# Feed-forward gate and up projections as seven half-width products (one level of Strassen's scheme), with sums made by accumulating DMA

## Chip, cores and metric

One core of one Trainium2 chip runs the kernel. The metric is the time of one execution in device microseconds. Three timed runs of the kernel before gave 751.33, 752.55 and 753.04 us; their median is 752.55 us.

## What is computed

One block of a streaming encoder on 512 tokens of width 1024, in float32. The change touches the last two steps; attention and gates before them stay as they are.

```python
x = x + jnp.einsum('bsd,de->bse', merged, w_out[layer])

h2 = _rmsnorm(x, g_ffn[layer])
ff = jax.nn.silu(jnp.einsum('bsd,df->bsf', h2, w_ffn_gate[layer])) * \
    jnp.einsum('bsd,df->bsf', h2, w_ffn_up[layer])
x = x + jnp.einsum('bsf,fd->bsd', ff, w_ffn_down[layer])
```

`w_ffn_gate` and `w_ffn_up` are 1024 x 2816, `w_ffn_down` is 2816 x 1024.

## The kernel before

Activations lie transposed: 128 features on the partitions, 512 tokens along the row, so a matrix of width 1024 is 8 tiles (k-tiles). Each float32 factor is split in two float32r parts: ScalarE copies it into the high part (L86), VectorE subtracts that from the factor for the low part (L87). `mm3` (L204 to L206) multiplies with three matmuls: high by high, high by low, low by high.

Weights come through `Stream`: a 128 x 1024 tile is loaded by SyncE's queue into a `raw` slot (6 of them, 5 tiles ahead), split into `wh` and `wl` (4 slots each, 2 tiles ahead) and used for 24 matmuls of 128 x 128 weights by 512 tokens. The stages, in the order of time:

- attention, with projections that fill the gaps, and the branch projections;
- the output projection (w_out): eight columns d, 24 matmuls each. VectorE adds the residual (`xr`, L701), ScalarE scales the sum by `g_ffn` into `h2h` (L705), VectorE makes `h2l` (L706), ScalarE squares it (L709), GpSimd sums the squares (L713);
- the feed-forward: 22 pairs n; each is a gate tile and an up tile, 24 matmuls each. After the first gate tile a matmul of the squares with ones gives the norm; ScalarE takes the root (L722), VectorE the reciprocal `r2` (L723). Per pair VectorE multiplies gate and up by `r2` (L726, L728), ScalarE applies SiLU (L727), GpSimd multiplies the two (L729), and the result is split into `fh` and `fl`;
- the down projection: eight columns of 66 matmuls over the 22 tiles, residual added (L740), output stored (L741).

A scheduler sets the order of the instructions on each engine; each engine and each DMA queue then runs its own in that order. In PSUM there are two pools of four banks: `pc` and `pt` tiles rotate through one, all others through the other.

Of the kernel before, what the change touches and what calls it, by code (L numbers as in the profile page):

```python
# [42 lines left out]
def block_kernel(  # L43
# [22 lines left out]
    small = ctx.enter_context(tc.tile_pool(name="small", bufs=4))  # L66
# [17 lines left out]

    def split(h, l, src):
        a = nc.scalar.copy(out=h, in_=src)  # L86
        b = nc.vector.tensor_tensor(out=l, in0=src, in1=f(h), op=ALU.subtract)  # L87
        return a, b

    def pinned(instrs):  # L90
        for ins in instrs:
            tc.keep_in_program_order(ins)

    class Stream:
        AHEAD, SPLIT = 5, 2
# [58 lines left out]
    srcs += [w_out[d] for d in range(8)]
    for n in range(NF):
        srcs += [w_fg[n], w_fu[n]]
    for d in range(8):
        srcs += [w_dn[d, :, 0:1024], w_dn[d, :, 1024:2048], w_dn[d, :, 2048:2816]]

    ws = Stream(srcs)  # L160
# [41 lines left out]
    def mm3(ps, w, a, first, last):  # L202
        (wh, wl), (ah, al) = w, a
        nc.tensor.matmul(out=ps, lhsT=wh, rhs=ah, start=first, stop=False)  # L204
        nc.tensor.matmul(out=ps, lhsT=wh, rhs=al, start=False, stop=False)  # L205
        nc.tensor.matmul(out=ps, lhsT=wl, rhs=ah, start=False, stop=last)  # L206
# [38 lines left out]
    def full_ct(acts, **kw):  # L245
        ps = kw.pop("ps", None) or PS("pc")
        drain(proj_ct(ps, acts, **kw))
        return ps
# [443 lines left out]
        split(h, l, gA[d])  # L692
        mg.append((h, l))

    x2, h2 = [], []
    acc = None
    for d in range(8):
# [4 lines left out]
        x2.append(xr)  # L702
        h, l = B(F32R, "h2h"), B(F32R, "h2l")
        gc = g_ffn[:, d : d + 1]
        nc.scalar.activation(out=h, in_=xr, func=AF.Copy, scale=gc)  # L705
        nc.vector.scalar_tensor_tensor(out=l, in0=xr, scalar=gc, in1=f(h), op0=ALU.mult, op1=ALU.subtract)  # L706
        h2.append((h, l))
# [9 lines left out]
    for n in range(NF):
        pg = full_ct(h2)
        if n == 0:
            pn = PS("pn2")  # L720
            nc.tensor.matmul(out=pn, lhsT=ones[:, 0:P], rhs=acc, start=True, stop=True)
            nc.scalar.activation(out=r2, in_=pn, func=AF.Sqrt, scale=1.0 / D, bias=epst)  # L722
            nc.vector.reciprocal(out=r2, in_=r2)  # L723
        pu = full_ct(h2)
        t1, t2 = B(name="t1"), B(name="t2")
        nc.vector.tensor_tensor(out=t1, in0=pg, in1=r2, op=ALU.mult)  # L726
        nc.scalar.activation(out=t1, in_=t1, func=AF.Silu)  # L727
        nc.vector.tensor_tensor(out=t2, in0=pu, in1=r2, op=ALU.mult)  # L728
        nc.gpsimd.tensor_tensor(out=t1, in0=t1, in1=t2, op=ALU.mult)  # L729
# [12 lines left out]


# [60 lines left out]
```

## Time and profile before

| | us |
|---|---|
| median of three runs | 752.55 |
| profiled execution, first to last instruction (span) | 751.0 |
| TensorE busy (matmul) | 738.1 |
| VectorE busy | 431.8 |
| ScalarE busy | 325.1 |
| GpSimd busy | 103.0 |

The profile is of one execution; its span is the time from the first instruction to the last. Engines: PE is TensorE's matmuls, PEld its weight loads, DVE VectorE, ACT ScalarE, POOL GpSimd, SP SyncE. A duration that is given for a matmul overlaps with the next one's, so the distance between two starts tells what one costs.

### The profile page before, as it was taken

How to read it: one execution, taken by the hardware profiler on the slowest of the kernel's cores; microseconds unless marked ns; L12 is line 12 of the kernel's file. 1: busy time of each engine (PE TensorE's matmuls, PEld its weight loads, DVE VectorE, ACT ScalarE, POOL GpSimd, SP SyncE). 2: the span in 40 equal slices, each digit the busy share in tenths (PEclk: the TensorE clock that was granted, in tenths of full speed). 3: DMA queues.
4: the chain of work that ended last, by engine and by line, in shares of the span. 5: the costliest groups of instructions: out<-in, count | busy, mean ns of one | idle time of the engine just before them, and what ended most of it. 6: DMA issues, size and time to landing. Idle time of an engine off the chain costs nothing.

```text
span 751.0 us, 9018 instructions
## 1 busy us (share of the span) xinstructions
PE 738.1 (98%) x3406; PEld 611.6 (81%) x3406; DVE 431.8 (57%) x648; ACT 325.1 (43%) x514; POOL 103.0 (14%) x139
## 2 busy tenths in 40 slices
PE   8999999999989999999999999999999999999998
PEld 6887887888878878888888888888888888888886
DVE  5856877766687887987446454445545533232220
ACT  6633566877566676544444232323232222222110
POOL 0067000000023223300321011101101111000000
PEclk9999999999999999999999999999999999999999
DMA  8622121211121111244432322332232323333200
GB/s 316 218 98 84 59 83 56 81 61 58 57 84 43 46 39 42 73 152 170 161 120 84 113 84 93 105 103 94 85 112 86 98 83 105 103 118 117 64 14 29
DMA packets 23803, 71.12 MB, mean 95 GB/s; under 512 B 2768, under 2 KB 3408, under 8 KB 23760
## 3 DMA queue, kind: packets, MB, share of 16 engines
q1 hardware_dynamic: 23472, 70.40, 28.0%
q8 instruction: 27, 0.44, 0.2%
q10 hardware_dynamic: 288, 0.15, 0.1%
q14 instruction: 16, 0.13, 0.1%
HBM read 68.44 MB, written 2.10 MB: 94 GB/s over the span
## 4 chain that ended last, share of the span: by engine, by line
PE 89%; DVE 3%; POOL 3%; ACT 2%; issue 2%; DMA 0%; DVEq 0%; POOLq 0%; ACTq 0%
PE pc L204 24%; PE pc L205 24%; PE pc L206 24%; PE pt L221 6%; PE pk L221 3%; PE sc L395 1%; PE sc L394 1%; POOL qn L300 1%; DVE wl L87 1%; PE tb L400 1%; ACT wh L86 1%; PE ta L400 1%; PE av L555 1%; POOL qn L314 1%; PE av L556 1%
## 5 line engine op out<-in xcount | busy, mean ns | idle before, releaser
L86 ACT CAST wh<-raw 128x1024 fp32r<-128x1024 f32 (+2 forms) x136 | 130.9, 963 | 299.1 <-PE pc L205 165.4
L87 DVE TENSOR_TENSOR wl<-raw,wh 128x1024 fp32r<-128x1024 f32 (+2 forms) x136 | 172.7, 1270 | 105.3 <-ACT wh L86 101.2
L204 PE MATMUL pc<-h2h,wh 128*128 128x512 f32 x352 | 137.3, 390 | 0.0
L206 PE MATMUL pc<-h2h,wl 128*128 128x512 f32 x352 | 137.0, 389 | 0.0
L205 PE MATMUL pc<-h2l,wh 128*128 128x512 f32 x352 | 136.9, 389 | 0.0
L204 PE MATMUL pc<-hh,wh 128*128 128x512 f32 x192 | 76.6, 399 | 1.9 <-DVE vs L363 1.5
L205 PEld LDWEIGHTS pc<-h2l,wh 128*128 128x128 f32 x352 | 66.1, 188 | 14.1 <-issue 0.2
L204 PEld LDWEIGHTS pc<-h2h,wh 128*128 128x128 f32 x352 | 66.1, 188 | 14.0 <-issue 0.2
L206 PEld LDWEIGHTS pc<-h2h,wl 128*128 128x128 f32 x352 | 66.1, 188 | 13.5
L206 PE MATMUL pc<-hh,wl 128*128 128x512 f32 x192 | 75.5, 393 | 0.0
L205 PE MATMUL pc<-hl,wh 128*128 128x512 f32 x192 | 75.3, 392 | 0.0
L204 PE MATMUL pc<-fh,wh 128*128 128x512 f32 x176 | 68.5, 389 | 0.0
L205 PE MATMUL pc<-fl,wh 128*128 128x512 f32 x176 | 68.5, 389 | 0.0
L206 PE MATMUL pc<-fh,wl 128*128 128x512 f32 x176 | 68.5, 389 | 0.0
L729 POOL TENSOR_TENSOR t<-t,t 128x512 f32<-128x512 f32 x22 | 30.0, 1363 | 208.5 <-DVE t L728 121.0
L728 DVE TENSOR_TENSOR t<-pc,r 128x512 f32<-128x512 f32 x22 | 15.2, 691 | 67.0 <-PE pc L206 63.2
L204 PEld LDWEIGHTS pc<-hh,wh 128*128 128x128 f32 x192 | 36.4, 190 | 9.2 <-issue 1.7
L206 PEld LDWEIGHTS pc<-hh,wl 128*128 128x128 f32 x192 | 36.2, 189 | 7.8
L205 PEld LDWEIGHTS pc<-hl,wh 128*128 128x128 f32 x192 | 36.4, 190 | 6.7
L530 POOL TENSOR_SCALAR_AFFINE_SELECT om<-om 128x128 f32<-128x128 f32 x32 | 11.4, 356 | 210.4 <-DVE obl L87 138.3
L204 PEld LDWEIGHTS pc<-fh,wh 128*128 128x128 f32 x176 | 33.0, 188 | 6.9
L206 PEld LDWEIGHTS pc<-fh,wl 128*128 128x128 f32 x176 | 33.0, 188 | 6.9
(204 smaller groups left out, 1166.4 us busy)
## 6 DMA issues: line engine op xcount, KB each, us to landing
raw<-w_fg_dram SPq DMA_DIRECT2D x22, 512.0 KB, 3.2
raw<-w_fu_dram SPq DMA_DIRECT2D x22, 512.0 KB, 3.2
raw<-w_gate_dram SPq DMA_DIRECT2D x16, 512.0 KB, 3.2
raw<-w_dn_dram SPq DMA_DIRECT2D x16, 512.0 KB, 3.5
raw<-w_tc_dram SPq DMA_DIRECT2D x12, 512.0 KB, 4.5
raw<-w_ct_dram SPq DMA_DIRECT2D x8, 512.0 KB, 3.3
raw<-w_br_dram SPq DMA_DIRECT2D x16, 256.0 KB, 2.6
raw<-w_out_dram SPq DMA_DIRECT2D x8, 512.0 KB, 3.3
```

Source lines behind the costliest of these rows:

```text
L86: a = nc.scalar.copy(out=h, in_=src)
L87: b = nc.vector.tensor_tensor(out=l, in0=src, in1=f(h), op=ALU.subtract)
L204: nc.tensor.matmul(out=ps, lhsT=wh, rhs=ah, start=first, stop=False)
L205: nc.tensor.matmul(out=ps, lhsT=wh, rhs=al, start=False, stop=False)
L206: nc.tensor.matmul(out=ps, lhsT=wl, rhs=ah, start=False, stop=last)
L221: nc.tensor.matmul(out=pss[tb], lhsT=hx[:, tb * P : (tb + 1) * P], rhs=wx[:, wsl], start=(kt == 0 and i == 0), stop=(kt == KT - 1 and i == 2),
L300: nc.gpsimd.tensor_tensor(out=q3, in0=q3, in1=gqkt[:, gi : gi + 1, :].broadcast_to([P, 8, 64]), op=ALU.mult,)
L314: nc.gpsimd.tensor_tensor(out=q3[:, :, 0:16], in0=t1, in1=t2, op=ALU.add)
L400: nc.tensor.transpose(out=ps[:, off + (tb - sb) * P : off + (tb - sb + 1) * P], in_=tiles[tb][:, sb * P : (sb + 1) * P], identity=ident,)
L530: nc.gpsimd.affine_select(out=t[:, o + w - P : o + w], in_=t[:, o + w - P : o + w], pattern=[[-1, P]], compare_op=ALU.is_gt, fill=fill, ba ...
L728: nc.vector.tensor_tensor(out=t2, in0=pu, in1=r2, op=ALU.mult)
L729: nc.gpsimd.tensor_tensor(out=t1, in0=t1, in1=t2, op=ALU.mult)
```

## The change

Gate and up tile of a pair are taken together. Tokens are halved (256 each), features are halved (4 k-tiles each), and the pair is a 2 x 2 block matrix with gate and up as its columns. Winograd's form of Strassen's scheme makes the four blocks of the result with seven products (`PRODUCTS`) where there are eight; each has 4 k-tiles x 3 matmuls on 256 tokens. In exchange sums are formed:

- of the activations, once, in the output projection's stage: `s13`, `s24`, beside the plain halves `a1x`, `a2x`. Its columns run in the order 0, 4, 1, 5, 2, 6, 3, 7; x after the residual goes to a scratch in DRAM and is read back for the end;
- of the weights, per pair: T1 and T3 (`t13`) by two plain loads of SyncE's queue and one accumulating DMA of GpSimd's queue from DRAM; T2 and T4 by VectorE (`sums`);
- of the products, by ScalarE (two copies) and VectorE (`c11`, `middle`, `c21`, `gate`).

For the up tile, and for the w_out tiles, the low part is no subtraction of VectorE: ScalarE writes the negated high part into `wl`, and an accumulating DMA of GpSimd's queue adds the raw tile to it. In the pair loop the order on TensorE, VectorE and ScalarE is the program's order. Pair 0 runs k-tiles 0 to 2 of all products first, then k-tile 3. `r2` multiplies the gate alone; the up part gets it at the very end (`yo`). GpSimd computes nothing there. All 22 results are split after the loop. `raw` has 5 slots in place of 6, `small` 3 in place of 4; weights are loaded 4 tiles ahead.

```diff
-N_BLK, N_RAW, N_SPLIT = 66, 6, 4
+N_BLK, N_RAW, N_SPLIT = 66, 5, 4
...
+    def split_dma(h, l, src):
+        nc.scalar.copy(out=h, in_=src)
+        nc.scalar.mul(out=l, in_=src, mul=-1.0)
+        nc.gpsimd.dma_start(out=l, in_=src, accum_op=ALU.add)
...
+        def load_t(self):
+            n = self.n
+            self.t13 = tsum.tile([P, 2 * S], F32, tag="t13", name=f"t13_{n}")
+            nc.sync.dma_start(out=self.t13[:, lo_w], in_=w_fu[n, :, lo_w])
+            nc.sync.dma_start(out=self.t13[:, hi_w], in_=w_fg[n, :, hi_w])
+            nc.gpsimd.dma_start(
+                out=self.t13.rearrange("p (a b) -> p a b", b=S),
+                in_=w_fg[n, :, lo_w].unsqueeze(1).broadcast_to([P, 2, S]), accum_op=ALU.add,
+            )
...
+        def sums(self):
+            self.t2, self.t4 = B(name="tb2"), B(name="tb4")
+            tt(self.t2, self.t13[:, lo_w], self.g)
+            tt(self.t4, self.t2, self.u[:, hi_w])
...
+    PRODUCTS = {
+        1: ("b11", "a11"), 2: ("b21", "a12"), 5: ("t1", "s1"), 7: ("t3", "s3"),
+        6: ("t2", "s2"), 4: ("t4", "a22"), 3: ("b22", "s4"),
+    }
+
+    def product(ps, pair, i, kts=range(KT // 2)):
+        w, x = PRODUCTS[i]
+        wh, wl = pair.of(w)
+        for kt in kts:
+            sl = slice(kt * P, (kt + 1) * P)
+            mm3(ps[:, 0:half], (wh[:, sl], wl[:, sl]), x_of[x](kt), kt == 0, kt == KT // 2 - 1)
...
+            if n == 0:
+                for i in PRODUCTS:
+                    product(o.ps(i), w, i, range(3))
+                for i in PRODUCTS:
+                    product(o.m[i], w, i, range(3, 4))
+                pn = PS("pn2")
+                nc.tensor.matmul(out=pn, lhsT=ones[:, 0:P], rhs=acc, start=True, stop=True)
+                nc.scalar.activation(out=r2, in_=pn, func=AF.Sqrt, scale=1.0 / D, bias=epst)
+                nc.vector.reciprocal(out=r2, in_=r2)
+            else:
+                product(o.ps(1), w, 1)
+                prev.gate()
+            if w1:
+                w1.sums()
+            if prev:
+                prev.mul()
+            o.copy(1, lo_t)
+            if n:
+                product(o.ps(2), w, 2)
+            o.c11()
+            if w1:
+                w1.prep_13()
+                w1.prep_g()
+            if n:
+                product(o.ps(5), w, 5)
+            o.copy(5, hi_t)
+            if w2:
+                w2.load_g()
+            if n:
+                product(o.ps(7), w, 7)
+                product(o.ps(6), w, 6)
+            o.middle()
+            if w1:
+                w1.high_24()
+            if n:
+                product(o.ps(4), w, 4)
+            o.c21()
+            if w1:
+                w1.low_24()
+            if n:
+                product(o.ps(3), w, 3)
+            if w2:
+                w2.prep_u()
+            if w3:
+                w3.load_u()
+            prev = o
...
+    for t in ff:
         h, l = B(F32R, "fh"), B(F32R, "fl")
-        split(h, l, t1)
-        ff.append((h, l))
+        split(h, l, t)
+        fs.append((h, l))
...
+            nc.vector.tensor_tensor(out=yo[:, sl], in0=ps[:, sl], in1=r2[:, sl], op=ALU.mult)
+            nc.vector.tensor_tensor(out=xr[:, sl], in0=yo[:, sl], in1=xr[:, sl], op=ALU.add)
```

Three places show what the order on the engines becomes. The first is SyncE's queue in the output projection's stage. `xr` is the residual's tile from `xT`, `raw` a weight tile; before, with what each row waits for (the names of semaphores of engines and DMA queues, DMASW being GpSimd's):

```order
L107 DMA raw_3646<-w_fu_dram 128x1024 [waits DMAHW3_49,DVE_49]
L699 DMA xr_3476<-xT_dram 128x512 [waits PE_49]
L107 DMA raw_3687<-w_fg_dram 128x1024 [waits DMAHW4_49,DVE_49]
L699 DMA xr_3516<-xT_dram 128x512 [waits PE_49]
L107 DMA raw_3728<-w_fu_dram 128x1024 [waits DMAHW5_49,DVE_49]
L699 DMA xr_3557<-xT_dram 128x512 [waits DMAHW6_49,Pool_49]
L699 DMA xr_3598<-xT_dram 128x512 [waits DMAHW7_49,PE_49]
```

The same place with the change, where `ru` and `rg` are raw up and gate tiles of the first pairs:

```order
L811 DMA xr_3557<-xT_dram 128x512 [waits DMAHW5_49,PE_49]
L751 DMA ru_3692<-w_fu_dram 128x1024 [waits DMAHW6_49,DMASW4_49,Activation_49]
L831 DMA x_scratch<-xr_3557 128x512 [waits DMAHW7_49,DVE_49]
L751 DMA ru_3744<-w_fu_dram 128x1024 [waits DMAHW0_49,DMASW6_49,Activation_49]
L811 DMA xr_3609<-xT_dram 128x512 [waits DMAHW1_49,PE_49,Pool_49]
L831 DMA x_scratch<-xr_3609 128x512 [waits DMAHW2_49,DVE_49]
L746 DMA rg_3859<-w_fg_dram 128x512 [waits DMAHW3_49,DMASW7_49,Activation_49]
L811 DMA xr_3658<-xT_dram 128x512 [waits DMAHW4_49,PE_49]
```

The next `xr` load stands behind a store of the one before and behind weight loads that wait for an accumulating DMA.

The second place is VectorE at the head of the feed-forward. Before, around the reciprocal of the norm:

```order
L87 TENSOR_TENSOR wl_3913<-raw_3769,wh_3912 128x1024
L723 RECIPROCAL r_3803<-r_3803 128x512
L726 TENSOR_TENSOR t_3870<-pc_3804,r_3803 128x512
L728 TENSOR_TENSOR t_3871<-pc_3839,r_3803 128x512
L87 TENSOR_TENSOR wl_3954<-raw_3809,wh_3953 128x1024
```

With the change (`t_1` is `t13` of pair 1, `pq` and `pc` products of pair 0, `wla` and `wlb` low parts of pair 1's sums):

```order
L919 RECIPROCAL r_3915<-r_3915 128x512
L705 TENSOR_TENSOR tb_4032<-t_1_3787,rg_3859 128x512
L705 TENSOR_TENSOR tb_4033<-tb_4032,ru_3744 128x512
L705 TENSOR_TENSOR t_3932<-pq_3947,pe_3929 128x256
L88 TENSOR_TENSOR wla_4039<-t_1_3787,wha_4038 128x1024
L88 TENSOR_TENSOR gl_4043<-rg_3859,gh_4042 128x512
L705 TENSOR_TENSOR uu_3930<-pc_3977,pe_3929 128x256
```

The first read of a product of pair 0 that frees a bank of the second pool stands behind the reciprocal and the two sums.

The third place is VectorE at the end of the feed-forward. Before, in the last pairs:

```order
L726 TENSOR_TENSOR t_5382<-pc_5320,r_3803 128x512
L728 TENSOR_TENSOR t_5383<-pc_5351,r_3803 128x512
L87 TENSOR_TENSOR wl_5454<-raw_5325,wh_5453 128x1024
L87 TENSOR_TENSOR fl_5389<-t_5382,fh_5388 128x512
L87 TENSOR_TENSOR wl_5481<-raw_5356,wh_5480 128x1024
```

With the change, where `fl` with the lowest number is the first pair's:

```order
L88 TENSOR_TENSOR fl_6927<-t_3931,fh_6926 128x512
L88 TENSOR_TENSOR wl_7084<-raw_7025,wh_7083 128x1024
L705 TENSOR_TENSOR t_6810<-pc_6902,t_6810 128x256
L88 TENSOR_TENSOR fl_6931<-t_4069,fh_6930 128x512
L705 TENSOR_TENSOR t_6810<-t_6810,r_3915 128x512
L88 TENSOR_TENSOR fl_6935<-t_4207,fh_6934 128x512
L88 TENSOR_TENSOR fl_6939<-t_4345,fh_6938 128x512
L705 TENSOR_TENSOR t_6810<-t_6810,t_6811 128x512
L88 TENSOR_TENSOR fl_6943<-t_4483,fh_6942 128x512
```

The low parts of all 22 results stand in a row, from the first pair's on, with the last gate between them.

## Rows read from the trace of the kernel before

**Rows 1.** The page: span, and section 4, the chain that ended last, by line:

```profile
span 751.0 us, 9018 instructions
...
PE pc L204 24%; PE pc L205 24%; PE pc L206 24%; PE pt L221 6%; PE pk L221 3%; PE sc L395 1%; PE sc L394 1%; POOL qn L300 1%; DVE wl L87 1%; PE tb L400 1%; ACT wh L86 1%; PE ta L400 1%; PE av L555 1%; POOL qn L314 1%; PE av L556 1%
```

**Rows 2.** Table by stage: us; busy (count) of PE, PEld, DVE, ACT, POOL; PEclk, DMA share, GB/s:

```profile
343.00:387.00 44.00, 44.00 (x195) 36.24 (x194) 23.52 (x29) 18.00 (x24) 9.96 (x6) 1.00 0.46 157
387.00:627.00 240.00, 240.00 (x1058) 198.35 (x1058) 119.64 (x111) 74.91 (x91) 30.47 (x22) 1.00 0.29 95
627.00:751.00 124.00, 120.40 (x532) 99.36 (x530) 31.85 (x33) 21.78 (x23) 1.29 (x1) 1.00 0.24 76
```

**Rows 3.** Timeline of TensorE, both ends of the feed-forward: start, duration, instruction:

```profile
387.29 0.39 PE L204 MATMUL pc<-h2h,wh 128*128 128x512 f32 x1
...
627.56 0.39 PE L204 MATMUL pc<-fh,wh 128*128 128x512 f32 x1
```

**Rows 4.** Timeline of TensorE, attention scores:

```profile
87.06 0.28 PE L394 MATMUL sc<-skh,sq 128*128 128x256 f32 x1
...
87.42 0.28 PE L395 MATMUL sc<-skl,sq 128*128 128x256 f32 x1
87.54 0.40 PE L204 MATMUL pc<-hh,wh 128*128 128x512 f32 x1
```

**Rows 5.** Timeline of VectorE, first pairs of the feed-forward; brackets: idle before, and releaser:

```profile
395.83 3.35 DVE L723 RECIPROCAL r<-r 128x512 f32<-128x512 f32 x1 [0.78 <-ACT r L722]
399.21 0.69 DVE L726 TENSOR_TENSOR t<-pc,r 128x512 f32<-128x512 f32 x1
399.82 0.68 DVE L728 TENSOR_TENSOR t<-pc,r 128x512 f32<-128x512 f32 x1
400.42 1.22 DVE L87 TENSOR_TENSOR wl<-raw,wh 128x1024 fp32r<-128x1024 f32 x1
...
411.06 2.30 DVE L87 TENSOR_TENSOR wl<-raw,wh 128x1024 fp32r<-128x1024 f32 x1 [0.21 <-ACT wh L86]
```

**Rows 6.** Timeline of VectorE, last pairs and end of the kernel:

```profile
623.38 0.95 DVE L87 TENSOR_TENSOR wl<-raw,wh 128x768 fp32r<-128x768 f32 x1
...
747.44 0.76 DVE L740 TENSOR_TENSOR xr<-pc,xr 128x256 f32<-128x256 f32 x2 [14.27 <-PE pc L206]
```

**Rows 7.** Timeline of GpSimd, beside the long subtraction of rows 5:

```profile
411.00 1.29 POOL L729 TENSOR_TENSOR t<-t,t 128x512 f32<-128x512 f32 x1 [7.54 <-DVE t L728]
```

**Rows 8.** Timeline of ScalarE, output projection and head of the feed-forward:

```profile
365.55 1.05 ACT L86 CAST wh<-raw 128x1024 fp32r<-128x1024 f32 x1 [2.53 <-issue]
366.51 0.73 ACT L705 ACTIVATE h2h<-xr,colt 128x512 fp32r<-128x512 f32 x1
367.15 0.61 ACT L709 ACTIVATE x2s<-xr 128x512 f32<-128x512 f32 x1
...
395.10 0.69 ACT L722 ACTIVATE r<-pn,epst 128x512 f32<-128x512 f32 x1
```

**Rows 9.** ScalarE's groups by shape: count, busy us, mean ns, idle before and releasers:

```profile
L727 ACT ACTIVATE t<-t 128x512 f32<-128x512 f32 x22 | 13.8, 626 | 1.4 <-DVE t L726 1.4
...
L86 ACT CAST tc<-tc 128x256 fp32r<-128x256 f32 x12 | 4.5, 376 | 4.5 <-PE tc L400 4.5
```

**Rows 10.** DMA from 387 to 627 us: queue; issues, KB each, median us to landing:

```profile
q1 hardware_dynamic: 6345, 22.70, 28.5%
...
raw<-w_fg_dram SPq DMA_DIRECT2D x17, 512.0 KB, 3.2
```

**Rows 11.** Timeline of TensorE, two waits in the attention:

```profile
70.49 0.33 PE L436 MATMUL qk<-ident,qn 128*128 128x128 f32 x1 [1.51 <-POOL qn L314]
...
219.22 0.61 PE L400 MATMUL ta<-ident,be 128*128 128x128 f32 x3 [2.35 <-DVE be L538]
```

**Rows 12.** Table of the stretches behind these two waits, columns as in rows 2:

```profile
219.60:223.00 3.40, 3.40 (x12) 2.86 (x11) 2.43 (x5) 2.95 (x5) 0.33 (x2) 0.50 0.40 148
70.50:75.00 4.50, 4.50 (x21) 3.73 (x21) 2.79 (x5) 2.90 (x5) 0.00 (x0) 1.00 0.32 117
```

More of the change, by code (lines that the diff above doesn't have):

```diff
@@ L132, in next @@
             self.at += 1
-            if i >= KT // 2:
-                for j in range(i, i + self.SPLIT):
+            if i >= self.own:
+                for j in range(i, i + self.SPLIT + (i >= self.dma_from - 1)):
                     self.split(j)
@@ L153, in block_kernel @@
     srcs += [w_br[d, 0] for d in range(8)]
[L154 to L160, printed above, removed]
+    srcs += [w_out[d] for d in (0, 4, 1, 5, 2, 6, 3, 7)]
+    wd = Stream(
+        [w_dn[d, :, a:b] for d in range(8) for a, b in ((0, 1024), (1024, 2048), (2048, 2816))]
+    )
+    ws = Stream(srcs, own=KT // 2, dma_from=len(srcs) - 8)
     xts = []
@@ L225, in proj_tc, with proj_ct @@
             yield
-    def proj_ct(ps, acts, first=True, last=True):
-        wh, wl = ws.next()
+    def proj_ct(ps, acts, first=True, last=True, stream=None):
+        wh, wl = (stream or ws).next()
         n = len(acts)
@@ L693, in block_kernel, with tt, __init__, put @@
         mg.append((h, l))
-    x2, h2 = [], []
-    acc = None
-    for d in range(8):
+    half = S // 2
+    lo_t, hi_t = slice(0, half), slice(half, S)
+    lo_w, hi_w = slice(0, S), slice(S, 2 * S)
+    def tt(o, a, b, op=ALU.add):
+        nc.vector.tensor_tensor(out=o, in0=a, in1=b, op=op)
+    class Operands:
+        def __init__(self, name):
+            self.h = [B(F32R, name + "h") for _ in range(KT // 2)]
+            self.l = [B(F32R, name + "l") for _ in range(KT // 2)]
+        def put(self, k, src):
+            split(self.h[k], self.l[k], src)
+        def at(self, i):
+            sl = (lo_t, hi_t)[i]
+            return lambda k: (self.h[k][:, sl], self.l[k][:, sl])
@@ new lines, in block_kernel @@
+    PRODUCTS = {
+        1: ("b11", "a11"), 2: ("b21", "a12"), 5: ("t1", "s1"), 7: ("t3", "s3"),
+        6: ("t2", "s2"), 4: ("t4", "a22"), 3: ("b22", "s4"),
+    }
+    def product(ps, pair, i, kts=range(KT // 2)):
[4 more added lines that the diff above has]
+            mm3(ps[:, 0:half], (wh[:, sl], wl[:, sl]), x_of[x](kt), kt == 0, kt == KT // 2 - 1)
+    pairs = [Pair(n) for n in range(NF)]
+    x2d = nc.dram_tensor("x2_scratch", (KT, P, S), F32, kind="Internal").ap()
@@ L700, in block_kernel @@
         ps = full_ct(mg)
-        nc.vector.tensor_tensor(out=xr, in0=ps, in1=xr, op=ALU.add)
[L702 to L707, printed above, removed]
+        if j == 2:
+            pairs[0].load_t()
+            pairs[0].load_g()
+        if j == 3:
+            pairs[0].load_u()
+        if j == 4:
+            pairs[1].load_u()
+        if j == 5:
+            pairs[1].load_t()
+            pairs[0].prep_u()
+            pairs[0].prep_13()
+        if j == 6:
+            pairs[0].sums()
+            pairs[0].prep_g()
+            pairs[0].high_24()
+            pairs[0].low_24()
+            pairs[1].load_g()
+        nc.vector.tensor_tensor(out=xr, in0=ps, in1=xr, op=ALU.add)
+        nc.sync.dma_start(out=x2d[d], in_=xr)
+        if d < 4:
+            uv = tsum.tile([P, 2 * S], F32, tag="t13", name=f"uv{d}")
+        k = d % 4
+        y = uv[:, (d // 4) * S : (d // 4 + 1) * S]
+        nc.scalar.activation(out=y, in_=xr, func=AF.Copy, scale=g_ffn[:, d : d + 1])
         sq = B(name="x2s")
         nc.scalar.activation(out=sq, in_=xr, func=AF.Square)
+        if d < 4:
+            split(a1x.h[k][:, lo_t], a1x.l[k][:, lo_t], y[:, lo_t])
+        else:
+            sa, sb = B(name="sa"), B(name="sb")
+            u_lo, u_hi, v_lo, v_hi = (uv[:, i * half : (i + 1) * half] for i in range(4))
+            tt(sa[:, lo_t], v_hi, u_hi, ALU.subtract)
+            tt(sa[:, hi_t], u_lo, u_hi, ALU.subtract)
+            s13.put(k, sa)
+            nc.vector.scalar_tensor_tensor(
+                out=sb[:, lo_t], in0=sa[:, lo_t], scalar=-1.0, in1=u_lo, op0=ALU.mult, op1=ALU.subtract
+            )
+            nc.vector.scalar_tensor_tensor(
+                out=sb[:, hi_t], in0=v_lo, scalar=-1.0, in1=sb[:, lo_t], op0=ALU.mult, op1=ALU.subtract
+            )
+            s24.put(k, sb)
+            a2x.put(k, y)
         if acc is None:
@@ L712, in block_kernel @@
         else:
-            nc.gpsimd.tensor_tensor(out=acc, in0=acc, in1=sq, op=ALU.add)
+            tt(acc, acc, sq)
     r2 = B(name="r2")
     ff = []
[L717 to L729, printed above, removed]
+    pairs[1].prep_u()
@@ new lines, in block_kernel @@
+    ET = mybir.EngineType
+    prev = None
+    with tc.manual_schedule(engines={ET.PE, ET.DVE, ET.Activation}):
+        for n in range(NF):
+            w, o = pairs[n], Out()
+            w1 = pairs[n + 1] if n + 1 < NF else None
+            w2 = pairs[n + 2] if n + 2 < NF else None
+            w3 = pairs[n + 3] if n + 3 < NF else None
+            if w3:
+                w3.load_t()
+            if n == 0:
[7 more added lines that the diff above has]
+                nc.vector.reciprocal(out=r2, in_=r2)
+            else:
+                product(o.ps(1), w, 1)
[31 more added lines that the diff above has]
+                w2.prep_u()
+            if w3:
+                w3.load_u()
+            prev = o
+        prev.gate()
+        prev.mul()
@@ L730, in block_kernel @@
+    wd.split(0)
+    fs = []
+    for t in ff:
         h, l = B(F32R, "fh"), B(F32R, "fl")
-        split(h, l, t1)
-        ff.append((h, l))
+        split(h, l, t)
+        fs.append((h, l))
     for d in range(8):
-        ps = full_ct(ff[0:8], last=False)
-        full_ct(ff[8:16], ps=ps, first=False, last=False)
-        full_ct(ff[16:22], ps=ps, first=False, last=True)
+        xr = B(name="xo")
+        nc.sync.dma_start(out=xr, in_=x2d[d])
+        ps = full_ct(fs[0:8], last=False, stream=wd)
+        full_ct(fs[8:16], ps=ps, first=False, last=False, stream=wd)
+        full_ct(fs[16:22], ps=ps, first=False, last=True, stream=wd)
```

92 lines of the change are left out of this document (84 added, 8 removed).

## The prediction

> **What bounds the kernel now.** I read the page's busy shares and chain first, then the table by stage, then TensorE's own start times. The chain that ended last runs almost wholly over the three matmul lines of `mm3` [rows 1], and in the projection, feed-forward and down stages TensorE is busy without a gap at full clock [rows 2]. Its stated durations (0.39 us) are pipelined; what a matmul costs is the distance from start to start. From the first gate matmul at 387.29 us to the first down matmul at 627.56 us it is 240.3 us [rows 3] for 22 pairs of 2 x 8 x 3 = 1056 matmuls of 512 columns and one normalising matmul, so 0.227 us each. VectorE has 50% of that stage, ScalarE 31%, the DMA engines 29% [rows 2]: only TensorE's count or a wait of TensorE's moves the end.
>
> **Fewer, but narrower matmuls.** A pair has now 7 products x 4 k-tiles x 3 = 84 matmuls of 256 columns, 1848 in all. What one costs is the largest term, and not half of 0.227 by itself, because each still brings a weight load of 128 columns. The trace has fp32r matmuls of 256 columns with a weight load each: the scores of the attention. Four in a row start from 87.06 to 87.42, and the next matmul at 87.54 [rows 4], 0.12 us each. Half of the 512-column distance, 0.1134, is the lower bound. I take 0.12, since the new stream is nothing but such matmuls: 1848 x 0.12 = 221.8, plus some 0.8 us for the normalising matmul, 222.6. Against 240.3 that is **-17.7 us** (-29.8 at 0.1134).
>
> **Do the other engines keep up in a pair of 84 x 0.12 = 10.1 us?** VectorE's work is one subtraction of 1024 columns, seven operations of 512 and seven of 256. A 512 takes 0.69 alone and 0.61 in a queue (399.21, 399.82, 400.42), a 1024 takes 1.22, and two 256s take 0.76 [rows 5, 6]: 1.22 + 7 x 0.61 to 0.69 + 7 x 0.38 = 8.2 to 8.7 us. The 2.30 us of a 1024 at 411.06 stood beside the multiplication on GpSimd at 411.00 [rows 5, 7]; that multiplication is gone from the pair loop, so I don't count it. ScalarE: three passes of 1024 at 1.05, four of 512 at 0.63, two of 256 at 0.38 [rows 8, 9], 6.4 us. Both fit, and weights are prepared a pair ahead, so half a pair of lag costs TensorE nothing. DMA: 22.7 MB took 28.5% of 240 us [rows 10], 3.0 us per MB on all engines. A pair loads 1.31 MB plainly (3.9 us) and accumulates 2 x 0.52 MB. No row shows an accumulating DMA. Priced as copies they are 3.2 us, 7.1 of 10.1; at twice that price 10.3. Nearest is the copy, so I take 0 and keep what lies above for a rival. The low part of an up tile has from the end of ScalarE's pass, about 0.7 us into the pair before, some 9 us to land, against 3.2 us for a load of that size [rows 10].
>
> **The head of the feed-forward, first wait.** Pair 0 runs k-tiles 0 to 2 of all products first, 63 x 0.12 = 7.6 us that cover the last projection column. Behind that column ScalarE has in its order: two passes over the up tile of pair 1, which wait for the slot of the last projection weight (2.1 us), then for columns 3 and 7 two scalings (0.72 each), two squares (0.61 each), a copy of 256 (0.38) and three of 512 (0.62 each), and VectorE the last low part (0.69): 7.7 us [rows 8, 9]. Between them VectorE's differences and low parts (one 512, four 256) add about 1.8, so 9.5 against 7.6 + 0.4. The order on SyncE adds to it: the `xr` loads now stand behind loads of `ru` and `rg` that wait for a free slot, which is there when the accumulating DMA of a w_out tile has landed: a slot of TensorE's, two passes of ScalarE (2.1 us) and a landing later, so `xr` comes some 3 us after the projection that it is added to. TensorE doesn't wait for `xr`, but ScalarE's last chain shifts by 1 to 2 us. I take **+3.0** (0 to 5). The w_out tiles themselves, split by ScalarE and a DMA, are asked for two tiles ahead; 24 x 0.227 = 5.4 us a tile cover 2.1 us and a landing, 0.
>
> **Second wait.** The order of VectorE puts the reciprocal (3.35 us [rows 5]), two sums and `c11` behind the normalising matmul; only `c11` frees the bank that product 2 of pair 1 writes (the fourth bank of that pool holds the normalising sum). From that matmul: square root 0.69 [rows 8], 3.35, 2 x 0.61, 0.38 and some 0.3 between engines make 5.9 us. TensorE can fill 1.44 us of it with product 1, once ScalarE's copy has freed that bank. In the kernel before the same reciprocal stood beside free banks and TensorE went on. **+4.6** (2.5 to 6).
>
> **The clock.** After a wait that shows 2.35 us idle, 3.4 us were granted at 0.50, 1.2 GHz [rows 11, 12]; after one of 1.51 us the clock stayed at 1.00. Both waits above may be as long as the first. 3.4 us at half speed lose 1.7: **+1.7** (0 to 3.4).
>
> **The step to the down projection.** Before, each pair's two splits ran in the pair. Now 22 stand together at the end. TensorE eats a tile in 3 x 0.227 = 0.68, VectorE makes one in 0.61, but between the first and last stand a 1024 weight split before the second, the last gate's 0.38, 0.61 and 0.61, and two weight splits later (1.22 and 0.95 [rows 5, 6], some 0.08 less in a queue): 4.8 us more, less 21 x 0.07 that VectorE gains on TensorE and 0.3 of lead: **+3.0** (1.5 to 4.8). **The tail**: the last 0.76 us of VectorE [rows 6] become 1.5, **+0.8**. One `raw` and one `small` buffer less: the order up to w_out is the same on every engine, and loads land in 3.2 us [rows 10] four tiles ahead; 0 (to 1).
>
> **Sum**: -17.7 + 3.0 + 4.6 + 1.7 + 3.0 + 0.8 = -4.6 on a span of 751.0, 746.4. The three timed runs, 751.33 to 753.04, lie 0.3 to 2.0 above that span; from their median of 752.55 it is **747.9 us**, and with all terms at their ends 727 to 755.
>
> **Rivals.** (1) *The narrow matmul costs 0.1134*: half of the wide distance points there, the four in a row don't. 12.1 us less, 735.8. The Trainium skill ("TensorE: Matmul & The Clock Gate", Back-to-back issue gap and LDWEIGHTS) goes further: 256 / 2.4 + 2.5 = 109 ns, with a weight load of 107 ns beneath it. By that rule an estimate of the time is 727.6. The trace disagrees: 227 ns at 512 columns where it has 216, 120 at 256 where it has 109 [rows 3, 4]. (2) *The accumulating DMAs bound the pair*, the slower end: the queue on GpSimd holds two per pair, and SyncE, VectorE and TensorE wait for their landing. It decides from twice a copy's price, where DMA work passes 10.1 us; at 2.5 times a pair takes 3.9 + 7.9 = 11.8, and some 20 pairs add 35 us, 783. For it: no row prices such a DMA, and it is added to a share of 29%. Against: nine us of slack hide latency, so only throughput counts. The Trainium skill ("Collectives: The Full Stack", The bandwidth ceiling) says that an add in a DMA isn't slowed by the add but by its two source reads, at half a copy's rate. By that rule the estimate is 10.3 us a pair and 752 in all; no row here shows it. (3) *VectorE's order binds*: with every wait between engines in line a pair passes the old 10.9 us. The 1.4 to 1.9 us that are free speak against; at 11.2 us per pair it would be 772. (4) *The waits at both ends are at their upper bounds*: 755. (5) *The cut isn't one*, pairs still at 10.9 us: 13 us of waits come on top, 766; the count of 84 narrow matmuls speaks against it.
>
> **How the numbers follow.** A difference under 0.2% (1.5 us) can't be told from none here. Forecast (741 to 752) 0.48; rival 1 0.12; rival 2 0.18; rival 3 and 5 together 0.07; rival 4 (752 to 757) 0.15. Faster than 751.05: 0.12 and nearly all of the forecast, with a little of rival 2, 0.60. Within: 0.11. Slower: 0.29. The range 735 to 762 leaves out most of rival 2, rival 3 and 5, and the lower half of rival 1.
>
> **What would show it.** In the profile after: start-to-start distance of the feed-forward matmuls (0.120 or 0.113); start of pair 2 to start of pair 21 over 19 (10.1 us if TensorE bounds, and then no wait by TensorE on a DMA or VectorE there); idle before the k-tile 3 matmul of `a2`, and before product 2 of pair 1, with PEclk 0.5 behind; TensorE waiting for `fl` at the start of the down projection. The prediction is wrong if PE waits for `wlu` or VectorE for `t13` in every pair.

## The result: 13% slower, and the profile after

The changed kernel takes 850.77 us (median of four runs, 848.2 to 852.27), the kernel before, run beside it, 752.79 us. The ratio is 1.130 (95% interval 1.128 to 1.133). The prediction said 747.9 us, with a range of 735 to 762.

The page of the changed kernel, its span, busy times, DMA queues and chain (q0 is GpSimd's software queue, which carries the accumulating DMAs; it did not exist before):

```profile
span 846.3 us, 11328 instructions
...
PE 754.8 (89%) x4198; PEld 661.5 (78%) x4198; DVE 518.2 (61%) x922; ACT 411.9 (49%) x670; POOL 115.3 (14%) x162
...
q1 hardware_dynamic: 32112, 80.36, 29.0%
q0 software_dynamic: 10304, 27.27, 17.9%
...
PE 58%; DMA 20%; DVE 10%; issue 5%; POOL 4%; ACT 3%; SPq 1%; POOLq 0%; DVEq 0%; ACTq 0%
PE pc L211 13%; PE pc L209 13%; PE pc L210 13%; DMA wlu<-ru 10%; PE pt L226 6%; DMA t<-w_fg_dram 4%; DMA xr<-xT_dram 3%; PE pk L226 2%; PE pq L210 2%; PE pq L209 2%; PE pq L211 2%; DMA ru<-w_fu_dram 1%; DVE t L705 1%; DVE wlb L705 1%; PE sc L400 1%
```

The chain that was almost all matmuls [rows 1] is now 20% DMA, and the DMA named first is `wlu<-ru`, the low part of the up tile. The table by stage shows where (columns as in [rows 2]). The stretches are the output projection, pair 0, pair 1, pairs 2 to 21, and the down projection:

```profile
344.50:393.50 49.00, 44.60 (x193) 35.65 (x193) 17.20 (x29) 22.36 (x32) 6.89 (x8) 1.00 0.87 225
393.50:432.30 38.80, 19.36 (x86) 16.31 (x86) 15.69 (x29) 14.63 (x25) 4.52 (x4) 0.69 0.62 152
432.30:446.70 14.40, 11.90 (x84) 11.70 (x85) 14.26 (x22) 10.02 (x16) 2.13 (x2) 0.88 0.58 145
446.70:721.40 274.70, 224.05 (x1683) 220.81 (x1681) 166.65 (x307) 120.27 (x180) 38.16 (x36) 0.90 0.69 168
721.40:846.30 124.90, 120.19 (x530) 98.88 (x528) 48.50 (x63) 30.86 (x42) 0.00 (x0) 0.99 0.31 97
```

The same table of the kernel before, for the output projection and the down projection:

```profile
343.70:387.30 43.60, 43.60 (x194) 35.89 (x193) 22.82 (x29) 18.00 (x24) 9.96 (x6) 1.00 0.46 157
...
627.60:751.00 123.40, 119.80 (x529) 98.88 (x527) 31.40 (x32) 21.67 (x23) 1.29 (x1) 1.00 0.24 76
```

The output projection takes 49.0 us where it took 43.6; the feed-forward 327.9 (38.8 + 14.4 + 274.7) where it took 240.3 [rows 3]; the down projection 1.5 us more. That is 5.4 + 87.6 + 1.5, and 0.8 ahead of them, for the 95.3 us between the spans.

The feed-forward's 327.9 us can be taken apart. Its matmuls are worth the 222.6 us that I had worked out: an undisturbed pair takes 10.08 us, 0.120 a matmul. Beyond that, pair 0 loses 38.8 - 10.9 = 27.9 us, pair 1 14.4 - 10.1 = 4.3, and pairs 2 to 21 lose 274.7 - 20 x 10.08 = 73 us, 13.7 us a pair. So seven tenths of the feed-forward's loss lie in the steady loop, in which I had expected none.

What TensorE waits for in the whole kernel (total, times, longest):

```profile
PE pc L211 <- DMA wlu<-ru: 51.8, 17, 5.4
PE pq L209 <- ACT a2h L87: 9.4, 2, 7.7
PE pc L209 <- DVE xr L830: 8.7, 3, 7.5
PE pc L211 <- DMA wl<-raw: 3.2, 2, 2.0
PE pc L211 <- DVE wla L88: 2.5, 1, 2.5
```

The first row is the loop, but for 1.1 us in pair 0; there are 16 waits in its 20 pairs, and the other four pairs take 10.1 us. The next three rows are the output projection and pair 0, the last is pair 1. Here is one turn of the loop, from the timelines of SyncE, GpSimd, ScalarE and TensorE (start, duration, instruction, idle time before it and its releaser):

```profile
516.36 1.05 ACT L93 ACTIVATE wlu<-ru 128x1024 fp32r<-128x1024 f32 x1
...
518.20 0.33 SPq L746 DMA_DIRECT2D rg<-w_fg_dram  x1
518.63 0.37 SPq L736 DMA_DIRECT2D t<-w_fu_dram  x1
519.05 0.42 SPq L737 DMA_DIRECT2D t<-w_fg_dram  x1
519.57 0.38 SPq L751 DMA_DIRECT2D ru<-w_fu_dram  x1
...
524.55 1.20 POOL L738 DMA_DIRECT2D t<-w_fg_dram  x1 [12.34 <-DMA ru<-w_fu_dram]
525.25 1.44 POOL L94 DMA_DIRECT2D wlu<-ru  x1
...
528.15 0.28 PE L210 MATMUL pc<-a1l,whu 128*128 128x256 f32 x1
533.55 0.58 PE L211 MATMUL pc<-a1h,wlu 128*128 128x256 f32 x1 [5.12 <-DMA wlu<-ru]
...
533.65 0.33 SPq L746 DMA_DIRECT2D rg<-w_fg_dram  x1
```

The chain that ended last has these landings too, with the engine's time between them (start, duration, what):

```profile
519.05 4.92 DMA t<-w_fg_dram
...
524.57 0.68 POOL t L738
525.25 8.26 DMA wlu<-ru
```

ScalarE has written the negated high part at 517.4, so the accumulating DMA of `wlu` could start there. It is issued at 525.25, because on GpSimd's queue it stands behind the accumulating DMA of `t13`, two pairs further on. That one waits for its two plain loads, issued at 518.63 and 519.05; the second lands 4.92 us later. (The row at 524.55 names `ru` as releaser, which is the profile's inference: `t13` isn't made from `ru`, and that load landed at 525.22, after the row's start.) The two loads stand on SyncE's queue behind the load of `rg`, which waits for a raw slot; and that slot is freed by the `wlu` of the pair before, in whose place `rg` is loaded. When `wlu` has landed at 533.5, TensorE starts and SyncE issues the next `rg`, 15.5 us after the last. The waits of SyncE in pairs 2 to 21 say the same:

```profile
SPq L746 <- DMA wlu<-ru: 205.1, 18, 13.9
```

It is a **ring**: wlu of pair n lands, `rg` of n+2 is loaded into its slot, `t13` of n+3 is loaded behind it (about 5 us), GpSimd issues its accumulating DMA and then `wlu` of n+1 (1.2 us), which takes about 8 us to land. About 14 us, once a pair. All but the issues is time in which DMAs land; no engine computes in it.

After such a wait TensorE also runs at half clock: from 533.50 to 537.00 the granted clock is 0.50 (1.2 GHz), and then 1.00.

```profile
533.50:537.00 3.50, 3.44 (x16) 3.45 (x17) 0.00 (x0) 0.37 (x1) 0.00 (x0) 0.50 0.62 180
537.50:543.00 5.50, 5.50 (x49) 5.50 (x48) 2.76 (x5) 3.03 (x5) 2.14 (x2) 1.00 0.63 162
```

Of the 73 us, 50.6 are waits for `wlu`; the rest is this clock, since TensorE is busy for 224.05 us there with matmuls that are worth 20 x 10.08 = 201.6. While the ring sets the period, a full clock should only lengthen the waits; that was argued, not tried.

### The profile page after: what moved, and what is told of

It is laid out like the page before. It is cut to its first block, busy times and chain, and to the rows that moved or that the text cites. A ratio compares the mean times of both kernels' runs of the same rounds, so it can differ in the third digit from the quotient of the medians.

```text
span 846.3 us, 11328 instructions
## 1 busy us (share of the span) xinstructions
PE 754.8 (89%) x4198; PEld 661.5 (78%) x4198; DVE 518.2 (61%) x922; ACT 411.9 (49%) x670; POOL 115.3 (14%) x162
## 4 chain that ended last, share of the span: by engine, by line
PE 58%; DMA 20%; DVE 10%; issue 5%; POOL 4%; ACT 3%; SPq 1%; POOLq 0%; DVEq 0%; ACTq 0%
PE pc L211 13%; PE pc L209 13%; PE pc L210 13%; DMA wlu<-ru 10%; PE pt L226 6%; DMA t<-w_fg_dram 4%; DMA xr<-xT_dram 3%; PE pk L226 2%; PE pq L210 2%; PE pq L209 2%; PE pq L211 2%; DMA ru<-w_fu_dram 1%; DVE t L705 1%; DVE wlb L705 1%; PE sc L400 1%
## 5 line engine op out<-in xcount | busy, mean ns | idle before, releaser
L87 ACT CAST wh<-raw 128x1024 fp32r<-128x1024 f32 (+2 forms) x84 | 76.1, 908 | 136.0 <-PE pc L210 91.7
L88 DVE TENSOR_TENSOR wl<-raw,wh 128x1024 fp32r<-128x1024 f32 (+2 forms) x84 | 88.8, 1059 | 72.9 <-ACT wh L87 64.9
L211 PE MATMUL pc<-a1h,wlu 128*128 128x256 f32 x88 | 32.2, 366 | 51.8 <-DMA wlu<-ru 51.8
L211 PEld LDWEIGHTS pc<-a1h,wlu 128*128 128x128 f32 x88 | 21.7, 246 | 55.2 <-DMA wlu<-ru 55.2
L738 POOL DMA_DIRECT2D t<-w_fg_dram x22 | 26.5, 1204 | 254.0 <-DMA ru<-w_fu_dram 149.1
L705 DVE TENSOR_TENSOR t<-pq,pe 128x256 f32<-128x256 f32 x22 | 9.3, 422 | 65.4 <-PE pq L211 55.5
L878 ACT COPY pe<-pc 128x256 f32<-128x256 f32 x44 | 16.3, 371 | 55.4 <-PE pc L211 55.4
L210 PEld LDWEIGHTS pc<-fl,wh 128*128 128x128 f32 x176 | 33.0, 188 | 7.4 <-DVE fl L88 0.5
L92 ACT CAST whu<-ru 128x1024 fp32r<-128x1024 f32 x22 | 23.1, 1049 | 31.3 <-issue 31.3
L209 PE MATMUL pq<-a2h,whu 128*128 128x256 f32 x88 | 29.4, 334 | 9.4 <-ACT a2h L87 9.4
```

The lines of the kernel that those rows point to most:

```text
L705: nc.vector.tensor_tensor(out=o, in0=a, in1=b, op=op)
L738: nc.gpsimd.dma_start(out=self.t13.rearrange("p (a b) -> p a b", b=S), in_=w_fg[n, :, lo_w].unsqueeze(1).broadcast_to([P, 2, S]), accum_op ...
L878: nc.scalar.copy(out=self.pe[:, sl], in_=self.m[i][:, 0:half])
```

## Experiments

Theory A was the ring. Rival B was what I had put down as a rival before: the DMA engines' work binds a pair. Rival C: VectorE's order does. Each time stands beside that of the kernel before on the same chip, 751.4 to 753.6 us; where no count is given it is a single run.

### The order of two queues, and nothing else

```diff
-    with tc.manual_schedule(engines={ET.PE, ET.DVE, ET.Activation}):
+    with tc.manual_schedule(engines={ET.PE, ET.DVE, ET.Activation, ET.Pool, ET.SP}):
```

> One edit: in the pair loop GpSimd's and SyncE's queues also keep the program's order; the same instructions on all engines, the same bytes. Theory A, a ring of waits through three queues: with the change, the low part of an up tile (wlu of pair n+1) stands on GpSimd's queue behind the accumulating sum T1/T3 of pair n+3, whose two plain loads stand on SyncE's queue behind the load of rg of pair n+2, which takes the slot that wlu of pair n frees: landing of the loads 4.8 us + issue 1.2 + landing of wlu 7.7 to 8.2, about 14 us for each pair. In program order the same ring closes over three pairs (4.8 us each), so the pair falls from 13.7 to between 10.1 (TensorE) and 10.9 us, and the time from 846 to 771-786. Rival B, throughput of the DMA engines binds a pair: 13.5 to 14.1 as before, 840-850. Rival C, VectorE's order binds a pair: no change either. Under B the DMA share stays at 0.70, under A it goes to 0.9 or more.

It takes 773.38 us (two runs), still 2.6% more than the kernel before; pairs 2 to 21 take 10.17 us on the mean, pair 2 11.8 and the others 10.08. In the steady stretch TensorE waits for nothing, and the DMA engines are nearly full. The table row and the queues' rows (the latter with packets, MB and share of 16 engines) of 460 to 640 us:

```profile
460.00:640.00 180.00, 180.00 (x1502) 180.00 (x1501) 145.13 (x268) 104.54 (x159) 34.86 (x33) 1.00 0.92 227
```

```profile
q0 software_dynamic: 6948, 17.83, 55.8%
q1 hardware_dynamic: 9624, 22.77, 36.1%
...
wlu<-ru POOLq DMA_DIRECT2D x17, 512.0 KB, 5.1
```

The same instructions move the same bytes, in 26% less time per pair (180 us for 1502 matmuls, 0.120 each). B and C fall: the DMA work does fit in a pair (0.92 x 10.08 = 9.3 us), and so does VectorE's (145.13 / 180 x 10.08 = 8.1 us).

### One place on one queue

The ring should open already when `wlu` moves up by one place on GpSimd's queue alone.

```diff
-    with tc.manual_schedule(engines={ET.PE, ET.DVE, ET.Activation}):
+    with tc.manual_schedule(engines={ET.PE, ET.DVE, ET.Activation, ET.Pool}):
```

What stands on GpSimd's queue in the change, and below it in this run:

```
L738 DMA t13_9_4761<-w_fg_dram 128x2x512
L94 DMA wlu7_4751<-ru7_4617 128x1024
L738 DMA t13_10_4899<-w_fg_dram 128x2x512
```

```
L738 DMA t13_9_4761<-w_fg_dram 128x2x512
L94 DMA wlu8_4889<-ru8_4755 128x1024
L738 DMA t13_10_4899<-w_fg_dram 128x2x512
```

> Of the two queues only GpSimd's keeps the program's order in the pair loop: wlu of pair n+2 stands behind T1/T3 of pair n+3 there, where in the change wlu of pair n+1 does; SyncE's queue keeps the order of the change, but for two loads. Theory A: the ring (wlu, rg, T1/T3, wlu) now closes over two pairs, 14.2 us for two, so one place on one queue is enough: 10.1 us a pair, 771-778. Rival: SyncE's order is needed as well, since rg of pair n+2 still stands ahead of T1/T3 of pair n+3 and waits for a landing there: 11 to 14 us a pair, 790-846.

It takes 778.87 us, a hair above what I had put down, and 10.5 us a pair. SyncE still waits for landings of `wlu` (the row of its waits from 450 to 640 us follows), but with a pair more to spare; TensorE waits 7.6 us in all, in nine places, where it waited 51.8.

```profile
SPq L746 <- DMA wlu<-ru: 138.9, 17, 11.8
```

### A sixth slot does not help

```diff
-N_BLK, N_RAW, N_SPLIT = 66, 5, 4
+N_BLK, N_RAW, N_SPLIT = 64, 6, 4
```

> Only the number of raw slots changes, six again as in the kernel before (two of the 66 blocks of 512 columns give the room), with two loads ahead of the loop moved by that. Theory A (ring): with six slots the load of rg no longer takes a slot of an up tile, but ru of pair m+3 takes that of ru of pair m, and in the order of the queues T1/T3 of pair m+3 stands behind that load on SyncE, and wlu of pair m+1 behind T1/T3 of pair m+3 on GpSimd: the ring still closes once in a pair, so the pair stays at 13 to 14.5 us and the time at 838-852. Rival: the missing slot is the cause, not the order: 10.1 us a pair, 770-782.

It takes 845.69 us, 13.8 us a pair. With six slots it is the load of `ru` (L751) that takes the slot of a `wlu` still to land, as SyncE's waits from 450 to 640 us show, and the ring is as short as before:

```profile
SPq L751 <- DMA wlu<-ru: 159.7, 14, 13.3
```

This speaks against the plainest reading of SyncE's waits, that a buffer was missing; more than six were not tried.

### The add taken out of the DMAs

```diff
-        nc.gpsimd.dma_start(out=l, in_=src, accum_op=ALU.add)
+        nc.gpsimd.dma_start(out=l, in_=src)
...
-                in_=w_fg[n, :, lo_w].unsqueeze(1).broadcast_to([P, 2, S]), accum_op=ALU.add,
+                in_=w_fg[n, :, lo_w].unsqueeze(1).broadcast_to([P, 2, S]),
```

> Both accumulating DMAs (sum T1/T3, low parts of w_out and up tiles) write plain copies in place of adding, from the same queue, with the same bytes and in the same order on every engine; the values are not those of the reference. Theory A (ring of 14 us, of which an accumulating landing is 7.7): the landing falls to 3-5 us, the ring to about 4.5 + 1.2 + 4 = 9.7, so TensorE binds at 10.1-10.9 us a pair; the software queue's work falls from 5.9 us a pair to about 3.2; time 765-785. Rival B (throughput): DMA work 9.9 to 7.2 us a pair, also 10.1, so the two differ here only by the price of a byte: if the add itself costs nothing, landing 7.7 and time 846 stay.

It takes 803.58 us, 12.0 us a pair: better by less than I had expected. Its DMA rows of 460 to 640 us:

```profile
q1 hardware_dynamic: 8640, 19.66, 33.3%
q0 software_dynamic: 4032, 14.68, 27.0%
...
t<-w_fg_dram POOLq DMA_DIRECT2D x15, 512.0 KB, 4.9
wlu<-ru POOLq DMA_DIRECT2D x15, 512.0 KB, 5.5
```

A plain `wlu` still takes 5.5 us to land, not 3 to 5, and the ring is shorter by 1.7 us a pair where the landing lost 2.2 (7.7 to 5.5). So the add's price lengthens the ring, but the ring stands without it. This run also prices the add. Here 1 MB costs 0.270 x 180 / 14.68 = 3.3 us on GpSimd's queue and 3.05 on SyncE's; with the add, in the run with both queues in order, 0.558 x 180 / 17.83 = 5.6 us against 2.85: 1.97 times a plain load beside it, and 1.7 times the plain copy on the same queue, which ran beside less other traffic.

### The up tile's low part by VectorE

```diff
-            split_dma(self.uh, self.ul, self.u)
+            split(self.uh, self.ul, self.u)
```

> The low part of the up tile is subtracted by VectorE (1.22 us a pair) as for the others; the sums T1/T3 stay with the accumulating DMA, w_out too. Theory A: the ring has no accumulating landing any more, the slot of ru is free after VectorE has read it, and the pair is bound by TensorE at 10.1 us (VectorE 9.4 to 9.9): 771-785. Rival C (VectorE's order binds): 1.2 us a pair more than 13.7, 870. Rival B: DMA work 9.9 less 2.9 is 7.0 us, 10.1 a pair as under A.

It takes 769.42 us; all pairs from pair 2 on take 10.08 us, without a wait, in the scheduler's own order of the queues. VectorE is at 92%, the DMA engines at 0.66 (stretch 460 to 640 us):

```profile
460.00:640.00 180.00, 180.00 (x1503) 180.00 (x1501) 165.76 (x289) 87.72 (x147) 17.89 (x15) 1.00 0.66 175
```

So the ring can be opened at either end, and VectorE had room for the subtraction that the DMA was to spare it.

### The head: w_out, xr, and the reciprocal

The head's loss is about 33 us. Its part in the output projection is due to the w_out tiles:

```diff
-    ws = Stream(srcs, own=KT // 2, dma_from=len(srcs) - 8)
+    ws = Stream(srcs, own=KT // 2, dma_from=len(srcs))
```

> Only the w_out tiles go back to VectorE's subtraction; the pair loop stays. Theory A for the head: the 6.2 us that the output projection lost and part of the 28 us of waits in pair 0 come from accumulating DMAs of w_out tiles (median 7.4 us to land) that stand on GpSimd's queue with T1/T3 of pair 0 and block SyncE's queue, and with it the loads of xr, through the slots that they hold: 6 to 16 us less, 830-840, pairs 2 to 21 unchanged at 13.7 us. Rival: xr waits for the loads of ru and rg alone, whose slots other tiles hold: 843-848.

It takes 842.19 us, 8.6 less, inside the 6 to 16 that I had put down, though as a time 2 us above 840. The output projection is back at 43.6 us, but pair 0 still loses 24 us. What holds pair 0 is seen in the changed kernel's timelines of SyncE and VectorE in that stage:

```profile
393.39 0.33 SPq L831 DMA_DIRECT2D x_scratch<-xr  x1
393.81 0.38 SPq L736 DMA_DIRECT2D t<-w_fu_dram  x1
394.25 0.44 SPq L737 DMA_DIRECT2D t<-w_fg_dram  x1
394.74 0.42 SPq L811 DMA_DIRECT2D xr<-xT_dram  x1
...
399.38 0.69 DVE L830 TENSOR_TENSOR xr<-pc,xr 128x512 f32<-128x512 f32 x1 [3.67 <-DMA xr<-xT_dram]
...
409.31 0.33 SPq L831 DMA_DIRECT2D x_scratch<-xr  x1
...
410.69 0.48 SPq L811 DMA_DIRECT2D xr<-xT_dram  x1
...
419.46 0.69 DVE L830 TENSOR_TENSOR xr<-pc,xr 128x512 f32<-128x512 f32 x1 [7.57 <-DMA xr<-xT_dram]
```

It is a second ring. The store of one column's result waits for VectorE's residual sum; the next `xr` load stands behind it on SyncE, lands 4 to 9 us later, and only then can VectorE add the next residual. The last residual comes at 419.46, 26 us after TensorE has begun pair 0. The test issues all eight loads first, on top of the order of the two queues:

```diff
+    xrs = {}
+    for d in (0, 4, 1, 5, 2, 6, 3, 7):
+        xrs[d] = B(name="xr")
+        nc.sync.dma_start(out=xrs[d], in_=xT[:, d])
     for j, d in enumerate((0, 4, 1, 5, 2, 6, 3, 7)):
-        xr = B(name="xr")
-        nc.sync.dma_start(out=xr, in_=xT[:, d])
+        xr = xrs[d]
```

> On top of the program's order on GpSimd's and SyncE's queue (773.4 us): all eight loads of xr are issued ahead of the output projection's columns. Theory A for the head: SyncE runs the store of column j, which waits for VectorE's residual sum of column j, ahead of the load of xr for column j+2 or j+1, so each residual waits for a load of 4 to 9 us that was asked for a column too late (VectorE waits 28 us for xr in that stage); with xr there the output projection loses nothing beyond its weights and pair 0's two long gaps (8.3 and 7.5 us) shrink to 1-3 us: 752-760. Rival B: the weights' accumulating DMAs set the head; the gaps move to wlu and wl: 768-774. Rival C: the chain of ScalarE and VectorE behind the last column sets it as I had forecast (3 us left of about 18): 758-764.

It takes 747.59 us, 26 less, better than any of the three had it. Pair 0 falls from 35.7 to 12.1 us, of which 84 matmuls and the norm are 10.9. VectorE waits for `xr` once, at the start of the stage, where it waited 26.9 us in six places in the change and 28.1 in five with the order alone (rows of the change, then of this run):

```profile
DVE xr L830 <- DMA xr<-xT_dram: 26.9, 6, 8.5
```

```profile
DVE xr L833 <- DMA xr<-xT_dram: 8.6, 1, 8.6
```

The w_out edit on top of that:

> As the run before, and the low parts of the w_out tiles by VectorE in place of ScalarE and an accumulating DMA. From the run with that edit alone (842.2 against 850.8 and the first gate matmul 5.7 us earlier): 5 to 7 us less than the run before, 746-754. If with xr early the accumulating DMAs of w_out are hidden, no difference; if VectorE's 8 x 1.22 us come into the residual's way, 2-4 us more.

It takes 746.75 us (five runs, 744.72 to 749.2; ratio to before 0.992, 0.989 to 0.995). The output projection gains 4.8 us, but pair 2 loses 1.7 of them to a 2.9 us wait for `wlu`; the times, one of them a single run, do not tell the two kernels apart.

The reciprocal's place, on top of the order of the queues alone:

```diff
-                nc.vector.reciprocal(out=r2, in_=r2)
...
             if w1:
                 w1.low_24()
+            if n == 0:
+                nc.vector.reciprocal(out=r2, in_=r2)
```

> On top of the program's order on both queues (773.4 us): the reciprocal of the norm (3.35 us on VectorE) stands behind pair 1's sums, splits and pair 0's combination instead of ahead of them. My theory of the second wait: TensorE's 2.8 us wait for the low part wla of pair 1 and the half clock behind it come from the reciprocal; pair 1 goes from 14.3 to 10.1-11.5 us, 769-771. Rival: the chain is held by the loads, which come late in the head anyway (wla waits for t13): 773.

It takes 773.09 us, a time that can't be told from 773.38. In the profiles the reciprocal's part is seen: pair 1 falls from 14.3 to 11.0 us and its wait for `wla` is gone. Pair 3 gives back 1.0 by a wait for `wlu`, and pair 2 is 0.6 shorter, so the feed-forward is 2.7 us shorter; the stages ahead of the output projection were 1.8 us longer in that execution. The mechanism is as I had it, and its price is within what one run can't show. The same edit on top of the order, the early `xr` and the w_out edit:

> All four edits: program's order on both queues, xr early, w_out's low parts by VectorE, reciprocal late. If the seven products are worth what the matmul count says (222.6 us against 240.3) and only the ring, the head and the reciprocal took it back: 742-750, faster than the kernel before. If the head's chain on ScalarE and VectorE stays at 8 us or more: 751-756.

It takes 745.86 us (four runs; ratio 0.991, 0.988 to 0.993), and again pair 1 gains 2.0 us (11.0 for 13.0), of which pair 2 gives 1.0 back (14.2 for 13.3).

### What is left when no wlu is waited for

The order of the queues, early `xr`, and the low parts of w_out and up tiles by VectorE, without the reciprocal's move and with it:

> Program's order on both queues, xr early, low parts of w_out tiles and of up tiles by VectorE; only T1 and T3 come from an accumulating DMA. Against the run with the same edits but the up tile's low part by DMA (746.8 us, pairs 1 and 2 at 13.0 and 13.3 us, the second by a 2.9 us wait for wlu): pair 2 falls to 10.1, 741-745. Rival, VectorE (9.4 to 9.9 us a pair) falls behind after the reciprocal: pairs 2 to 5 at 10.5 to 11, 745-749.

> The run before, with the reciprocal behind pair 1's sums and splits. If a wait that is taken away in pair 1 is kept once no wlu is waited for (with the wlu by DMA it came back in pair 2, 14.2 in place of 13.3 us): 2 us less than the run before, 739-743. Rival: the 3.35 us come back as a late gate or late weights, since VectorE has only 0.2 to 0.7 us to spare in a pair: no difference, or up to 2 us more.

They take 741.55 us (four runs; ratio 0.987, 0.984 to 0.989) and 740.34 us (four runs; ratio 0.984, 0.982 to 0.986). Both beat the kernel before, by 1.3 and 1.6%. In the first, pair 2 falls from 13.3 to 10.1 us, as put down, and pair 1 stays at 13.0. In the second, pair 1 takes 12.1 us and all later pairs 10.1 to 10.2. The late gate costs 1.6 us there, so a part of the reciprocal came back, as the rival had it, and a part stayed. Only T1 and T3 are left of the accumulating DMAs.

## Why the prediction was wrong

- **Narrow matmuls: right.** A pair is 10.08 us, 0.120 a matmul, to the last digit of the four attention scores [rows 4]. The 0.1134 of rival 1 never showed. Nor did the 109 ns that the Trainium skill's formula gives for a single matmul of 256 columns, without its weight load ("TensorE: Matmul & The Clock Gate", Back-to-back issue gap). Rival 5 falls with it: the cut is one. The -17.7 us are there wherever the loop doesn't wait; the best kernel keeps 11.6 of them.
- **"Do the other engines keep up": the step that failed.** VectorE and ScalarE were sized right (8.1 and 5.9 us measured, 8.2 to 8.7 and 6.4 forecast). The sentence on the `wlu` was not: "The low part of an up tile has from the end of ScalarE's pass ... some 9 us to land". It took for granted that the DMA is issued when its data is ready. On GpSimd's queue it stood 7.8 us behind `t13`. I had looked at SyncE's queue and at VectorE's order in the head, and for the loop had counted bytes and busy times only. "nine us of slack hide latency, so only throughput counts" is true of a chain that is open; this one was closed, and in a ring the latencies add up and set the period. This cost 73 us. With both queues in the program's order the slack is there: a `wlu` is issued at 528.10 for a pair that starts at 537.19.
- **Rival 2: the right symptom, the wrong cause.** TensorE waits for `wlu` in 16 of 20 pairs, which I had named as the mark of DMA throughput. The DMA engines were at 0.69 then, and at 0.92 without a wait once the order had changed. Its price was about right: with the add 1 MB takes 1.97 times a plain load's time, and rival 2 was to decide from twice; at 9.3 us of DMA work in a pair of 10.08 it just does not. The Trainium skill ("Collectives: The Full Stack", The bandwidth ceiling) has half a copy's rate for an add, measured on collectives. The traces come near it, at 1.97 times a plain load beside it and 1.7 times a copy on the same queue. I had priced the sum at the copy.
- **First wait: right place, far too small.** I had `xr` 3 us late once, for +3.0 (0 to 5). It was late at six of eight columns, since each load stood behind the store of the column before. With the w_out tiles, the head lost 5.4 + 27.9 us. For these tiles I had 0, since 5.4 us a tile were to cover two passes of ScalarE (2.1 us) and a landing; the landing alone took 7.4 us (median).
- **Second wait: right cause and size, wrong place.** +4.6 (the addends make 4.5) and a share of the clock forecast; pair 1 lost 4.3 us, and the move of the reciprocal took 3.3 of them away. But I had TensorE wait for the bank that `c11` frees before product 2. Product 2 starts at 433.86, ahead of `c11` at 436.58; what waits is product 5, for `wla`, which stands behind the reciprocal on VectorE as well. That the size fits is in part luck (rows of the change, TensorE and VectorE):

```profile
433.86 0.28 PE L209 MATMUL pq<-a2h,whu 128*128 128x256 f32 x1
...
438.18 0.45 PE L211 MATMUL pc<-sah,wla 128*128 128x256 f32 x1 [2.48 <-DVE wla L88]
...
436.58 0.42 DVE L705 TENSOR_TENSOR t<-pq,pe 128x256 f32<-128x256 f32 x1
```

- **The clock: right in kind.** 3.5 us at 0.50 follow a long wait, but there was such a wait in most pairs of the loop and not only at the head.
- **The step to the down projection and the tail: too high.** +3.8 forecast, +1.5 measured; TensorE waited for no `fl` beyond 0.5 us.
- **Rival 3** falls: VectorE at 92% still let TensorE run without a wait. **Rival 4**, the waits at both ends at their upper bounds, was too low for the head, which lost 33 us where the first wait's bound was 5, and too high for the end; with the loop mended and the head as it was, the time was 773, not 755.

## To carry to other kernels

Before counting busy time, follow the queues around: for every DMA that an engine issues in order, ask what stands ahead of it, what that waits for, and whether the walk comes back to a buffer that this same DMA frees. If it does, the latencies on the way, divided by the number of rounds that the walk spans, are a lower bound of the period, and neither a free engine nor one more slot need change it. An order left to a scheduler on a queue that only issues DMAs is as much a part of the critical path as the order on TensorE.

## What the runs showed of the hardware

An accumulating DMA took 5.6 us a MB on all engines where plain loads beside it took 2.85, and a plain copy through the same queue 3.3. One that wrote 512 KB landed in 5 to 8 us (medians of 5.1 for `wlu` and 8.1 for `t13` with both queues in order, 7.7 and 6.4 in the change; in each of the two the slower is the one that is issued second). GpSimd's issue of one shows 1.20 to 1.44 us in the change's rows above, SyncE's of a plain load 0.33 to 0.48. With the DMA engines at 0.92 TensorE did not wait.
